# One-core decoder step: the last four projection columns in halves, two attention units begun amid them

## The chip, the cores and the metric

The kernel runs on one core of one Trainium2 chip. The time is that of the device for one execution, in microseconds (us). Names of engines: PE is the matrix unit (TensorE), PEld its weight loads, DVE VectorE, ACT ScalarE, POOL GpSimd, SP SyncE, which here issues DMA transfers. PSUM is the memory that PE writes to, eight banks of 128 x 512 floats; SBUF is the memory of the tiles.

## The reference

One step of a hybrid decoder layer, for a prompt of 1024 tokens and eight sample tokens that decode one position each, all in float32. One projection feeds three groups of heads (attention with three branches, an RWKV-7 recurrence, attention into 256 memory rows); each group is gated, and one more projection and the residual close the layer:

```python
q_raw, kv_raw, g_raw, z_nsa, u_rw, z_rw, q_mem, z_mem = split_in(rms_norm(hp, ln_g[l]) @ w_in[l])
q, rows4, rows_w = nsa_project(q_raw, kv_raw, pos_p, nsa_q_norm[l], nsa_k_norm[l])
gates = jax.nn.sigmoid(g_raw).reshape(bp, tp, NSA_HEADS, 3)
o_nsa = lax.map(lambda a: nsa_prompt_seq(*a, *cmp_params), (q, rows4, rows_w, gates))
o_rw, sh_p, st_p = rwkv7_mix(u_rw, ...)
mkv_p = mem_kv(mem_prompt, mem_norm_g[l], w_mem_kv[l], mem_k_norm[l])
o_mem = mem_attend(q_mem, mkv_p, mem_q_norm[l])
hp = hp + mixer_out(o_nsa, z_nsa, o_rw, z_rw, o_mem, z_mem, w_out[l])
```

The attention group is, for a block of 128 queries, `gate_mix(g, o_c, o_s, o_w)`: a softmax over compressed keys (`o_c`), one over selected blocks of keys (`o_s`), one over a window of 512 (`o_w`). `mem_kv` is `rms_norm(mem, g) @ w_kv`, with one more norm per head on its keys. `mixer_out` multiplies each group by `silu` of its `z` columns. The sample tokens go through the same with a cache.

## The kernel before

Products that need float32 are made from split operands: a weight block is loaded as `wraw`, ACT rounds it to `whi` and DVE subtracts to `wlo` (`w_split`, L283 and L284); three matmuls (`h`, low part of `h`, `wlo`) make one product. `wraw` and the split pair have two buffers each (pools `wr`, `wp`).

**Phase 1** multiplies the 1024 tokens with `w_in`, 128 columns at a time (`columns`, then `project`, L307). A column has two halves of tokens: H=0 with tokens 0 to 511 and the eight sample tokens (24 matmuls of 256 and 24 of 264 columns), H=1 with 512 to 1023 (24 of 512). Both use the same split block. Results land in the PSUM pool `ppr` (3 banks). The last four columns are `z` columns: `do_z` makes `zt` on ACT (L318) and DVE (L319) and writes it to `z_d` in DRAM by SP (L320). While these four run, a generator `bg`, made by `ahead`, is stepped: BG = 6 steps of it for each 8 steps of a column. `ahead` makes the compressed keys (`prompt_cmp`), the memory's keys and values (`mem_kv`: `p_mT` L1090, four raw blocks of `w_mem_kv` with their split L1099 to L1103, products `p_mo` L1110 in the PSUM pool `pw`, then a norm and transfers, L1116 to L1119), the attention keys `kh` and `kl`, and the queries `qs` of tile 7.

**Phase 2** goes over units (tile i of 128 queries, group g, head pair hp), tile 7 first, 32 units. `attn_scores` makes the scores `p_s` of two heads and two branches on PE, in the PSUM pool `pS` (2 buffers of 2 banks). `weigh` subtracts the maximum on DVE (L1356, which leaves `p` and `nm`) and takes the exponential on ACT (L1357); POOL multiplies by gate over sum (L1382). `attn_turn` transposes `p` on PE to `p_pT` (3 banks `pT`), copied to `pt` by ACT (L1327) or DVE (L1329) in turn; `attn_out` multiplies with the values. Scores run two units ahead, so the phase begins with those of units 0 and 1, `start`. Beside the units run other generators, among them `query_tasks`: for tile 7 the compressed branch `attn_cmp` (scores `p_sc`, weights `pcq` on DVE L1292 to L1304, their transpose), for each further tile the queries: `q` loaded by SP (L1254), split on ACT and POOL (`qhl`, L1259 and L1260), transposed on PE (`p_q`), copied to `qs`. `sample_tasks` makes the sample tokens' work (`s_in`, `s_x`, `p_sn`).

**Phase 3** is the output projection. The order of instructions on each engine is set by the framework's scheduler from the order of the code, with priorities (`first`, `high_priority`); on an engine they then run in that order, and each waits for what it reads and for the last use of the memory that it writes. Pools that are closed give their memory to pools opened later, so a tile can wait for the last use of another that lay there.

The two places in `phase1` and `phase2` that matter are the loop over `late` and `bg`, and `start = chain(scores(0), scores(1))`.

## Time and profile before

| | us |
|---|---|
| three runs | 965.71, 967.79, 972.04 (median 967.79) |
| the profiled execution | 966.81 |
| its span in the profile | 965.0 |
| PE busy in it | 926.7 (96 %) |
| DVE, ACT, POOL busy | 653.2, 441.6, 179.3 |
| mean granted clock of PE | 0.994 of full speed |

A row of the timeline gives start, duration, engine, line, operation, output and input with its shape; in brackets stands how long the engine had been idle before it and what ended that. The rows of PE are modelled at their ends, so those that run back to back overlap in print. L and a number is a line of the kernel.

### The profile page before, as it was taken

Reading aid. Unit: us, or ns where it says so; the run is one execution under the profiler, and the core shown is the slowest. Engines: PE = TensorE matmul, PEld = TensorE weight load, DVE = VectorE, ACT = ScalarE, POOL = GpSimd, SP = SyncE. Lnnn points to the kernel's source line nnn. Section 1 sums busy time; section 2 is a strip of 40 time slices with the busy share of each in tenths; the row PEclk is TensorE's granted clock in tenths of the full one; section 3 lists DMA queues with packets and bytes.
Section 4 is the critical chain, followed back from the end, with each engine's and each line's share of the span. In section 5 each row is a group of like instructions: output and inputs, shape, how many; then the busy total and the mean of one; then the engine's idle time right before and its main releaser. Section 6 shows DMA issues by size and latency. Waiting matters only on the chain.

```text
span 965.0 us, 24725 instructions
## 1 busy us (share of the span) xinstructions
PE 926.7 (96%) x9845; PEld 787.8 (82%) x9845; DVE 653.2 (68%) x2025; ACT 441.6 (46%) x990; POOL 179.3 (19%) x270
## 2 busy tenths in 40 slices
PE   8999999999999998999998999999999998999998
PEld 8998888868888887778886887888888877887875
DVE  6668579846593897653447765766777996457474
ACT  7564324333432332223435666567576666224321
POOL 2000000000000000000103435344355755211010
PEclk9999999999999999999999999999999999999999
DMA  8421314211331126146337425141210036976611
GB/s 273 130 66 45 90 28 128 78 48 55 88 100 36 40 77 164 46 112 153 97 99 210 144 68 180 45 140 33 61 40 14 27 110 178 326 242 211 208 71 42
DMA packets 133964, 103.82 MB, mean 108 GB/s; under 512 B 34705, under 2 KB 121240, under 8 KB 133720
## 3 DMA queue, kind: packets, MB, share of 16 engines
q1 hardware_dynamic: 128888, 90.53, 31.9%
q0 software_dynamic: 3200, 10.49, 3.0%
q8 instruction: 78, 1.28, 0.5%
q10 hardware_dynamic: 1760, 1.21, 0.4%
q14 instruction: 38, 0.31, 0.1%
HBM read 83.61 MB, written 22.78 MB: 110 GB/s over the span
## 4 chain that ended last, share of the span: by engine, by line
PE 72%; DVE 14%; ACT 5%; DMA 4%; issue 3%; SPq 1%; POOL 0%; DVEq 0%; ACTq 0%; POOLq 0%
PE p_pr L87 22%; PE p_out L87 9%; PE p_pr L307 6%; PE p_s L87 5%; PE p_pT L87 4%; PE p_o L87 4%; ACT p L1357 2%; DVE p L1356 2%; PE p_hid L87 2%; PE p_iy L87 2%; PE p_z L87 1%; PE p_it L87 1%; DVE pt L1329 1%; PE p_mo L1110 1%; PE p_tk L87 1%
## 5 line engine op out<-in xcount | busy, mean ns | idle before, releaser
L87 PE MATMUL p_pr<-h,whi 128*128 128x512 f32 (+5 forms) x1024 | 249.1, 336 | 0.0
L87 PEld LDWEIGHTS p_pr<-h,whi 128*128 128x128 f32 (+1 forms) x1024 | 162.3, 185 | 19.0 <-issue 2.8
L87 PE MATMUL p_pr<-h,wlo 128*128 128x512 f32 (+5 forms) x512 | 165.0, 325 | 0.6 <-DVE wlo L284 0.6
L1382 POOL TENSOR_SCALAR p<-p,fac,gates 128x640 f32<-128x640 f32 (+7 forms) x128 | 104.1, 825 | 107.3 <-DVE fac L1379 61.1
L1357 ACT ACTIVATE p<-p,nm 128x640 f32<-128x640 f32 (+7 forms) x128 | 93.0, 728 | 53.0 <-DVE nm L1356 46.6
L87 PEld LDWEIGHTS p_pr<-h,wlo 128*128 128x128 f32 (+1 forms) x512 | 93.9, 184 | 10.3 <-DVE wlo L284 0.8
L87 PE MATMUL p_pT<-ident,p 128*128 128x128 f32 x528 | 71.0, 279 | 4.9 <-ACT pt L1327 1.6
L1031 POOL MEMSET w2d<- 128x128 f32 x1 | 0.2, 206 | 394.2 <-PE p_yy L87 394.2
L1356 DVE CUSTOM_DVE_ANT_0 p<-p_s,bmask 128x512 f32<-128x512 f32 (+7 forms) x96 | 60.3, 661 | 18.5 <-PE p_s L87 18.0
L87 PEld LDWEIGHTS p_pT<-ident,p 128*128 128x128 f32 x528 | 57.0, 141 | 15.8 <-issue 6.4
L87 PE MATMUL p_s<-kh,qs 128*128 128x512 f32 (+3 forms) x191 | 66.8, 361 | 2.0 <-DVE nm L1356 1.9
L307 PE MATMUL p_pr<-h,whi 128*128 128x264 f32 (+2 forms) x320 | 68.6, 309 | 0.0
L87 PE MATMUL p_o<-pt,vs 128*64 128x128 f32 x1056 | 67.9, 277 | 0.4 <-DVE cat L1415 0.4
L284 DVE TENSOR_TENSOR wlo<-wraw,whi 128x1024 fp32r<-128x1024 f32 (+1 forms) x34 | 40.7, 1197 | 37.0 <-ACT whi L283 37.0
L87 PEld LDWEIGHTS p_o<-pt,vs 128*64 128x64 f32 x1056 | 57.0, 137 | 7.2 <-issue 3.8
L87 PE MATMUL p_s<-kl,qs 128*128 128x512 f32 (+3 forms) x192 | 61.3, 339 | 0.0
L283 ACT ACTIVATE whi<-wraw 128x1024 fp32r<-128x1024 f32 (+1 forms) x35 | 36.4, 1039 | 48.9 <-PE p_pr L87 36.7
L1329 DVE COPY pt<-p_pT 128x512 f32<-128x512 f32 (+1 forms) x72 | 48.3, 673 | 14.0 <-PE p_pT L87 13.3
L307 PEld LDWEIGHTS p_pr<-h,whi 128*128 128x128 f32 x320 | 51.2, 189 | 3.0 <-ACT whi L283 0.5
L87 PE MATMUL p_out<-woh,chi 128*128 128x512 f32 x128 | 51.8, 405 | 0.0
L87 PE MATMUL p_out<-woh,clo 128*128 128x512 f32 x128 | 50.2, 392 | 0.4 <-DVE clo L2267 0.4
L87 PE MATMUL p_out<-wol,chi 128*128 128x512 f32 x128 | 49.9, 390 | 0.0
(549 smaller groups left out, 1932.6 us busy)
## 6 DMA issues: line engine op xcount, KB each, us to landing
wraw<-in_w_in_dram SPq DMA_DIRECT2D x34, 512.0 KB, 3.8
pg<-in_c_pool_dram SPq DMA_DIRECT2D x32, 256.0 KB, 6.4
pg<-in_c_pool_dram SPq DMA_DIRECT2D x48, 128.0 KB, 2.2
x<-in_x_prompt_dram SPq DMA_DIRECT2D x8, 512.0 KB, 7.1
z_d<-zt SPq DMA_DIRECT2D x16, 256.0 KB, 3.0
cat<-z_d SPq DMA_DIRECT2D x8, 512.0 KB, 5.2
xres<-in_x_prompt_dram POOLq DMA_DIRECT2D x16, 256.0 KB, 3.6
out_dram<-xres POOLq DMA_DIRECT2D x16, 256.0 KB, 3.0
```

The costliest lines, as they stand in the source:

```text
L87: self.last = getattr(self.engine, op)(*a, **k)
L283: nc.scalar.activation(hi[:, :, :n], raw[:, :, :n], AF.Copy)
L284: (low or nc.vector).tensor_tensor(lo[:, :, :n], raw[:, :, :n], hi[:, :, :n].bitcast(F32), op=OP.subtract)
L307: self.last_mm = self.pe.matmul(ps[:m, :b - a], w[:, k, :m], h[k][:, a:b], start=(k == 0 and i == 0), stop=(k == 7 and i == 2))
L1031: nc.gpsimd.memset(w2d[:], 0.0)
L1110: PE.matmul(po[t][:], a, w[:, j], start=(k + j == 0 and i == 0), stop=(k + j == 7 and i == 2))
L1329: nc.vector.tensor_copy(pt[:, :n], ps[:, :n])
L1356: V.tensor_tensor_reduce(halves(x), halves(ps), m, -1.0, 3.0e38, op0=OP.add, op1=OP.min, accum_out=nm[:, h, b:b + 1])
L1357: A.activation(x, x, AF.Exp, scale=-1.0, bias=nm[:, h, b:b + 1], accum_out=sm[:, h, b:b + 1])
L1382: nc.gpsimd.tensor_scalar(x, x, f[:, h, b:b + 1], gate[:, hd + h, 1 + b:2 + b], op0=OP.mult, op1=OP.mult)
```

## The change

- `halves` replaces `columns` for the last four columns: first halves (H=0) of all four, then second halves (H=1) of all four. A column's weight block is loaded and split anew for its second half. BG becomes 9.
- The tiles of `h` for H=0 lie in a pool of their own, `hp0`. When the four first halves and `ahead` are done, that pool, `wk1` and the PSUM pool `pw` are closed. In their place are opened the PSUM pool `p7` (1 buffer of 2 banks) and `pp` (the tiles `p`), and the scores of units 0 and 1 of tile 7 are made as further steps of `bg`, amid the second halves (`scores`, UNITS = 2). `start` has nothing left of them.
- `attn_cmp` is split into `cmp_weights` (scores and weights `pcq`) and `cmp_turn` (the transpose). For tile 7 the weights are made in `ahead` (`stacked`), and so are the sample's tables. The last multiplication of `pcq` is on POOL for every tile.
- `mem_kv` ends with one copy of both halves to `mrows`, one norm over eight heads and one transfer.

PE at the end of `mem_kv`, where its products (`p_mo`) stand among those of the last column (`p_pr`). Before:

```order
L1110 MATMUL p_mo<-whi,mhi_6820 128x512
L1110 MATMUL p_mo<-wlo,mhi_6820 128x512
L1110 MATMUL p_mo<-whi,mlo_6822 128x512
L307 MATMUL p_pr<-h_0_667,whi 128x512
L307 MATMUL p_pr<-h_0_668,whi 128x512
L307 MATMUL p_pr<-h_0_667,wlo 128x512
L307 MATMUL p_pr<-h_1_670,whi 128x512
L307 MATMUL p_pr<-h_1_671,whi 128x512
L307 MATMUL p_pr<-h_1_670,wlo 128x512
L1110 MATMUL p_mo<-whi,mhi_6820 128x512 x2
```

After, with the end of the first column's second half, and the first scores behind:

```order
L308 MATMUL p_pr<-h_7_916,wlo 128x512
L1145 MATMUL p_mo<-wlo,mhi_6864 128x512
L1145 MATMUL p_mo<-whi,mlo_6866 128x512
L1145 MATMUL p_mo<-whi,mhi_6864 128x512
L1145 MATMUL p_mo<-wlo,mhi_6864 128x512
L1145 MATMUL p_mo<-whi,mlo_6866 128x512
L1145 MATMUL p_mo<-whi,mhi_6865 128x512 x2
L1145 MATMUL p_mo<-wlo,mhi_6865 128x512
L1145 MATMUL p_mo<-whi,mlo_6867 128x512
L1145 MATMUL p_mo<-wlo,mhi_6865 128x512
```

The products of the raw blocks now stand behind one another up to their end, and no `p_pr` between them.

PE where the projections end. Before, the last `p_pr` is followed by 24 matmuls of `p_s` (with `kh` and `kl` in turn) and the 17 of `p_sc`; then stands this:

```order
L87 MATMUL p_pT<-ident,p 128x128 x16
L87 MATMUL p_s<-kh_6300,qs 128x128
L87 MATMUL p_s<-kl_6301,qs 128x128
L87 MATMUL p_s<-kh_6303,qs 128x512
L87 MATMUL p_s<-kl_6304,qs 128x512
L87 MATMUL p_sn<-s_x_7272,s_in_7257 128x64
L87 MATMUL p_sn<-ident,s_in_7259 128x8 x7
L87 MATMUL p_pT<-ident,pcq 128x128 x4
```

After, from the last four matmuls of the last column on:

```order
L308 MATMUL p_pr<-h_6_913,wlo 128x512
L308 MATMUL p_pr<-h_7_916,whi 128x512
L308 MATMUL p_pr<-h_7_917,whi 128x512
L308 MATMUL p_pr<-h_7_916,wlo 128x512
L88 MATMUL p_pT<-ident,p 128x128 x8
L88 MATMUL p_q<-ident,qhl 128x128 x4
L88 MATMUL p_pT<-ident,p 128x128 x10
L88 MATMUL p_s<-kh_6303,qs 128x512
```

The scores of units 0 and 1 and `p_pT<-ident,pcq` have moved ahead of the end of the projections; `p_q` (queries of tile 6) stands eight transposes behind it.

SP at the same place: `z_d<-zt` is the write of a finished column, `q<-q_d` the load of a tile's queries. Before:

```order
L320 DMA z_d<-zt 128x512
L1129 DMA kd<-out_dram 128x4x64
L1254 DMA q<-q_d 128x768
L1129 DMA kd<-out_dram 128x4x64
L1254 DMA q<-q_d 128x768
L1118 DMA out_dram<-nr_y 128x256
L1270 DMA y_rw<-y_d 128x256
L1271 DMA cat_7205<-z_d 128x8x128
```

After:

```order
L321 DMA z_d<-zt 128x512
L1824 DMA mxv_8132<-in_cache_mem_dram 128x2x256 x2
L321 DMA z_d<-zt 128x512
L1295 DMA q<-q_d 128x768 x2
L1311 DMA y_rw<-y_d 128x256
L1312 DMA cat_7335<-z_d 128x8x128
```

Both loads of `q` stand directly behind the last `z_d`, as before one did behind `z_d` and one `kd`; what changed is the work of the other engines that surrounds it: the last `zt` and the last `z_d` come when the attention has already begun. The tile of the first `pt` behind them on ACT lies in memory that held `zt`.

The diff:

```diff
--- before.py
+++ after.py
@@ -25,10 +25,11 @@
 XT = 2
 PTB = 8
 KB = 2
+UNITS = 2
 FREE = 0
 ORDER = [4, 1, 11, 2, 3, 6, 5, 7, 13, 17, 10, 9, 15, 8, 0, 12, 14, 18, 16, 19, 20]
 EARLY = 17
-BG = 6
+BG = 9
 STEP = 0.7
 SLACK = 1.3
 AHEAD = 400
@@ -245,7 +246,7 @@
-        return [self.hp.tile([128, W], F32R, name=f"h{p}{H}_{k}") for p in range(2)]
+        return [self.hp[H].tile([128, W], F32R, name=f"h{p}{H}_{k}") for p in range(2)]
...
@@ -460,10 +461,12 @@
         with ExitStack() as ctx:
             P = lambda name, bufs, **k: ctx.enter_context(tc.tile_pool(name=name, bufs=bufs, reuse_waits="tile", **k))
             self.small = P("small", 2)
-            self.hp = P("hp", 1)
+            hp1 = P("hp1", 1)
             self.ev = P("ev", 1)
             self.wr = P("wr", 2)
             self.wp = P("wp", 2)
+            hctx = ctx.enter_context(ExitStack())
+            self.hp = hctx.enter_context(tc.tile_pool(name="hp0", bufs=1, reuse_waits="tile")), hp1
             rctx = ctx.enter_context(ExitStack())
             PR = lambda name, bufs: rctx.enter_context(tc.tile_pool(name=name, bufs=bufs, reuse_waits="tile"))
             self.tk = PR("tk", 1)
@@ -474,7 +477,8 @@
             self.rp = R("rp", 1)
             self.ppr = P("ppr", 3, space=PSUM)
             self.ptr = P("ptr", 2, space=PSUM)
-            self.pw = P("pw", 3, space=PSUM)
+            pctx = ctx.enter_context(ExitStack())
+            self.pw = pctx.enter_context(tc.tile_pool(name="pw", bufs=3, reuse_waits="tile", space=PSUM))
             self.hi, self.lo = ([], []), ([], [])
             self.pe = self.te = nc.tensor
             with ExitStack() as xctx:
@@ -553,10 +557,25 @@
             self.rwkv_close()
             rctx.close()
             self.key_pools()
-            self.wk = self.tk = P("wk1", 1)
+            wctx = ctx.enter_context(ExitStack())
+            self.wk = self.tk = wctx.enter_context(tc.tile_pool(name="wk1", bufs=1, reuse_waits="tile"))
             self.pM = Tag(self.ptr, "tr")
-            bg = self.ahead()
-            late = self.columns(cols[EARLY:])
+
+            def scores():
+                while len(self.half) < len(cols[EARLY:]):
+                    yield
+                pctx.close()
+                wctx.close()
+                hctx.close()
+                self.p7 = P("p7", 1, space=PSUM)
+                self.pp = self.kctx.enter_context(tc.tile_pool(name="pp", bufs=4, reuse_waits="tile", side="right"))
+                for n in range(UNITS):
+                    yield from self.attn_scores(7, 0, n, self.begun[n])
+                self.p7 = None
+
+            self.begun, self.half = [{} for _ in range(UNITS)], []
+            bg = chain(self.ahead(), scores())
+            late = self.halves(cols[EARLY:])
             for _ in group(late, 8):
                 for _ in islice(bg, BG):
                     pass
@@ -572,7 +591,14 @@
             yield from self.q_stack(7)
 
         self.mem_x()
-        yield from weave(chain(self.prompt_cmp(), self.mem_kv()), keys())
+        def stacked():
+            while 7 not in self.qs:
+                yield
+            self.pc7 = self.slot(3, [128, 8, 64], F32, "pcq")
+            yield from self.cmp_weights(7, self.pc7)
+            self.tables = self.sample_tables()
+
+        yield from weave(chain(self.prompt_cmp(), stacked(), self.mem_kv()), keys())
 
     def drive(self, work, fill):
 
@@ -626,6 +652,15 @@
                 yield STEP
         if rest:
             rest()
+
+    def halves(self, tiles):
+
+        for H in range(2):
+            for c0, do, j in tiles:
+                out = []
+                yield from self.project(H, *self.wblock(c0, 128), 128, out)
+                do(H, out, j)
+                self.half.append(H)
 
     def last_u(self):
         nc, O = self.nc, self.O
@@ -1109,15 +1144,21 @@
                     for i, (a, w) in enumerate(((h, wh), (h, wl), (l, wh))):
                         PE.matmul(po[t][:], a, w[:, j], start=(k + j == 0 and i == 0), stop=(k + j == 7 and i == 2))
             yield
+        m = self.slot(6, [128, 2, 512], F32, "mrows")
+        for t in range(2):
+            A.activation(m[:, t], po[t][:], AF.Copy)
+        y = m[:, :, 0:256].rearrange("p t (h d) -> p t h d", d=64)
+        sq = self.slot(7, [128, 8, 64], F32, "nr_sq")
+        A.activation(sq[:].rearrange("p (t h) d -> p t h d", t=2), y, AF.Square)
+        ss = self.small.tile([128, 8], F32, name="nr_ss", tag="nrss8")
+        V.tensor_reduce(ss[:], sq[:], axis=AX.X, op=OP.add)
+        r = self.rsqrt(self.small, ss[:], 8, 1.0 / 64, 1e-6)
+        yield
+        V.tensor_tensor(y, y, bc(r.rearrange("p (t h) -> p t h", t=2)[:, :, :, None], [128, 2, 4, 64]), op=OP.mult)
+        V.tensor_tensor(y, y, bc(self.gains[:, 5:6, None, :], [128, 2, 4, 64]), op=OP.mult)
         dst = O["mem_kv_prompt"]
-        for t in range(2):
-            d0 = bass.AP(tensor=dst.tensor, offset=dst.offset + t * 128 * 512, ap=[[512, 128], [1, 512]])
-            mv = self.slot(2 + t, [128, 256], F32, f"mv{t}")
-            A.activation(mv[:], po[t][:, 256:512], AF.Copy)
-            kn = self.norm_rope(po[t][:, 0:256].rearrange("p (t c) -> p t c", t=1), 5, 1, 4, None)
-            nc.sync.dma_start(d0[:, 0:256], kn.rearrange("p h d -> p (h d)"))
-            nc.sync.dma_start(d0[:, 256:512], mv[:])
-            yield
+        nc.sync.dma_start(bass.AP(tensor=dst.tensor, offset=dst.offset, ap=[[512, 128], [128 * 512, 2], [1, 512]]), m[:])
+        yield
 
     def mem_keys(self):
 
@@ -1272,6 +1313,18 @@
 
     def attn_cmp(self, i):
 
+        pcq = self.we.tile([128, 8, 64], F32, name="pcq", tag="pcq")
+        yield from self.cmp_weights(i, pcq)
+        yield 7.0
+        yield from self.cmp_turn(i, pcq)
+
+    def cmp_turn(self, i, pcq):
+
+        self.pcT[i] = self.pt_copy(lambda j: pcq[:, 2 * j:2 * j + 2, :].rearrange("p a b -> p (a b)"), "c")
+        yield
+
+    def cmp_weights(self, i, pcq):
+
         nc = self.nc
         V, A, G, PE = nc.vector, nc.scalar, nc.gpsimd, self.te
         qs = self.qs[i]
@@ -1286,7 +1339,6 @@
                     PE.matmul(p2[:, j, g], qs[:, 4 * g + j, :], ck[:, 0, g * 64:g * 64 + 64], start=False, stop=(j == 3 and g == 1 and n == 1))
             if j == 1:
                 yield 0.1
-        pcq = self.we.tile([128, 8, 64], F32, name="pcq", tag="pcq")
         v3 = lambda x: x.rearrange("p a b c -> p (a b) c")
         st = self.small.tile([128, 8], F32, name="c_m")
         V.tensor_reduce(st[:], v3(p2[:]), axis=AX.X, op=OP.max)
@@ -1301,10 +1353,7 @@
         V.tensor_scalar(rc[:], sm[:], 1e-30, None, op0=OP.max)
         V.reciprocal(rc[:], rc[:])
         V.tensor_tensor(gh, gh, gate[:, :, 0].rearrange("p (g h) -> p g h", g=2), op=OP.mult)
-        (G if i < 7 else V).tensor_tensor(pcq[:], pcq[:], bc(rc[:, :, None], [128, 8, 64]), op=OP.mult)
-        yield 7.0 if i < 7 else 4.0
-        self.pcT[i] = self.pt_copy(lambda j: pcq[:, 2 * j:2 * j + 2, :].rearrange("p a b -> p (a b)"), "c")
-        yield
+        G.tensor_tensor(pcq[:], pcq[:], bc(rc[:, :, None], [128, 8, 64]), op=OP.mult)
 
     def attn_rwkv(self, i):
         cat = self.cat[i]
@@ -1364,7 +1413,7 @@
                 Ps[h, b] = self.pp.tile([128, 1024 if b == 0 else 640], F32, name="p", tag=f"p{b}")
             if split:
                 for h in range(2):
-                    ps = self.pS.tile([128, 1024], F32, name="p_s", tag="s")
+                    ps = (self.p7 or self.pS).tile([128, 1024], F32, name="p_s", tag="s")
                     scores(ps[:, c0:512], qs[:, hd + h, :], b, c0, 512)
                     scores(ps[:, 512:n1], qs[:, hd + h, :], b, 512, n1)
                     weigh(ps[:, c0:n1], h, b, c0)
@@ -1468,7 +1517,7 @@
 
     def query_tasks(self):
 
-        yield from self.attn_cmp(7)
+        yield from self.cmp_turn(7, self.pc7)
         self.done.add(("cmp", 7))
         for i in range(6, -1, -1):
             while i < 6 and (self.unit < 4 * (5 - i) + 2 or ("mem", i + 2) not in self.done):
@@ -1521,7 +1570,6 @@
             self.pT = P("pT", 3, space=PSUM)
             self.pO = P("pO", 1, space=PSUM)
             self.pM = Tag(self.pT, "t")
-            self.pp = P("pp", 4)
             self.load_z(7)
             self.te = nc.tensor
             self.attn_setup(P)
@@ -1532,7 +1580,7 @@
-            P = [{} for _ in units]
+            P = self.begun + [{} for _ in units[UNITS:]]
...
@@ -1582,9 +1630,9 @@
                 lag = lambda n: n + (2 if n < 15 else 3)
                 return [m for m in range(lag(n - 1) + 1, lag(n) + 1) if m < len(units)]
 
-            start = chain(scores(0), scores(1))
-            for k in range(6):
-                next(start)
+            start = chain(*(scores(n) for n in range(UNITS, 2)))
+            for k in range(2):
+                next(start, None)
                 slot()
             pts = turn(*groups[0])
             for _ in start:
@@ -1643,7 +1691,8 @@
-        return rows[:NS, 0:896].rearrange("p (k c) -> p k c", k=7)
+        self.nc.sync.dma_start(rows[:, 896:1024], self.I["c_rw"][:, 128:256])
+        return rows[:NS, 0:896].rearrange("p (k c) -> p k c", k=7), rows[:, 896:1024]
...
@@ -1659,9 +1708,7 @@
-        sums = self.slot(1, [128, 1024], F32, "s_in1")[:, 0:128]
-        nc.sync.dma_start(sums, I["c_rw"][:, 128:256])
-        rows = self.sample_tables()
+        rows, sums = self.tables
...
```

## The prediction

> **What bounds the kernel now.** I read the page first (span and busy times), then two-microsecond windows over the place where the projections end and attention begins, then the engines' timelines there.
>
> ```profile
> span 965.0 us, 24725 instructions
> PE 926.7 (96%) x9845; PEld 787.8 (82%) x9845; DVE 653.2 (68%) x2025; ACT 441.6 (46%) x990; POOL 179.3 (19%) x270
> ```
>
> TensorE (PE) works 926.7 of 965.0 us. The change leaves PE the same matmuls, so it can move only PE's idle time and the time PE runs at a lower clock. Columns of the windows: length, then busy time and count of PE, weight load, DVE, ACT, POOL, then granted clock, DMA share, GB/s.
>
> ```profile
> 508.00:510.00 2.00, 2.00 (x11) 1.59 (x9) 0.27 (x1) 0.93 (x3) 0.00 (x0) 1.00 0.31 25
> 512.00:514.00 2.00, 2.00 (x11) 1.60 (x10) 2.00 (x16) 0.77 (x4) 0.00 (x0) 1.00 0.20 67
> 516.00:518.00 2.00, 0.99 (x9) 0.86 (x7) 1.31 (x3) 0.00 (x0) 0.00 (x0) 1.00 0.36 120
> 518.00:520.00 2.00, 1.08 (x5) 0.65 (x6) 2.00 (x5) 1.24 (x2) 0.00 (x0) 1.00 1.00 270
> 520.00:522.00 2.00, 1.90 (x6) 1.08 (x7) 1.16 (x3) 1.49 (x4) 0.73 (x1) 0.59 0.95 279
> 522.00:524.00 2.00, 2.00 (x7) 1.22 (x6) 1.91 (x6) 2.00 (x7) 1.56 (x2) 0.56 1.12 339
> 524.00:526.00 2.00, 1.83 (x14) 1.43 (x13) 2.00 (x4) 1.07 (x4) 1.52 (x2) 1.00 1.03 255
> 526.00:528.00 2.00, 2.00 (x18) 1.58 (x17) 1.89 (x7) 2.00 (x4) 1.14 (x2) 1.00 0.99 260
> 528.00:530.00 2.00, 0.29 (x5) 0.19 (x4) 2.00 (x6) 1.61 (x5) 1.81 (x3) 1.00 1.05 346
> 530.00:532.00 2.00, 1.33 (x7) 1.36 (x8) 1.93 (x6) 0.21 (x1) 1.59 (x1) 0.65 0.93 292
> 532.00:534.00 2.00, 2.00 (x9) 1.70 (x9) 1.60 (x6) 0.46 (x2) 0.00 (x0) 0.50 0.80 248
> ```
>
> The last projection matmul ends near 513.2 us. From 516 to 534 PE is busy 0.99+1.08+1.90+2.00+1.83+2.00+0.29+1.33+2.00 = 13.42 of 18 us: 4.6 us idle. In 520 to 524 it runs at 0.59 and 0.56 of its clock, in 530 to 534 at 0.65 and 0.50: lost are 1.90 x 0.41 + 2.00 x 0.44 = 1.66 and 1.33 x 0.35 + 2.00 x 0.50 = 1.47, together 3.1 us. **This seam loses 7.7 us in all**, and that is all the change can win. PE's timeline names the waits:
>
> ```profile
> 512.80 0.39 PE L307 MATMUL p_pr<-h,wlo 128*128 128x512 f32 x1
> ...
> 518.73 0.33 PE L87 MATMUL p_s<-kh,qs 128*128 128x128 f32 x1 [1.74 <-DVE nm L1356]
> ...
> 524.88 1.89 PE L87 MATMUL p_pT<-ident,p 128*128 128x128 f32 x15 [0.17 <-POOL p L1382]
> ...
> 530.67 1.09 PE L87 MATMUL p_pT<-ident,pcq 128*128 128x128 f32 x4 [2.38 <-DVE pcq L1304]
> ...
> 532.83 1.05 PE L87 MATMUL p_q<-ident,qhl 128*128 128x128 f32 x4
> ```
>
> 1.74 us goes to the scores' buffer, which the softmax weighing on DVE (`nm`) frees late; 2.38 us to `pcq`, the compressed branch's weights, made in DVE's queue amid that weighing. DVE is busy 2.00 of 2.00 us in 518 to 520 and 524 to 526: too much of its work begins at once. Before the seam it is nearly free (0.27 of 2.00 in 508 to 510), and PE full. So the change moves work from a place where DVE is the bound to a place where PE is.
>
> **The change part by part.** Durations come from these rows.
>
> ```profile
> L87 PE MATMUL p_pr<-h,wlo 128*128 128x512 f32 (+5 forms) x512 | 165.0, 325 | 0.6 <-DVE wlo L284 0.6
> L284 DVE TENSOR_TENSOR wlo<-wraw,whi 128x1024 fp32r<-128x1024 f32 (+1 forms) x34 | 40.7, 1197 | 37.0 <-ACT whi L283 37.0
> L283 ACT ACTIVATE whi<-wraw 128x1024 fp32r<-128x1024 f32 (+1 forms) x35 | 36.4, 1039 | 48.9 <-PE p_pr L87 36.7
> ...
> wraw<-in_w_in_dram SPq DMA_DIRECT2D x34, 512.0 KB, 3.8
> z_d<-zt SPq DMA_DIRECT2D x16, 256.0 KB, 3.0
> cat<-z_d SPq DMA_DIRECT2D x8, 512.0 KB, 5.2
> ...
> 481.94 0.33 PE L1147 MATMUL p_k<-ident,kd 128*128 128x128 f32 x1 [0.57 <-POOL kd L1140]
> ...
> 513.23 0.60 ACT L318 ACTIVATE zt<-p_pr 128x512 f32<-128x512 f32 x1 [1.64 <-PE p_pr L307]
> 513.72 0.22 ACT L1669 ACTIVATE s_x<-t_s 128x32 f32<-128x32 f32 x1
> 514.18 0.26 ACT L1672 ACTIVATE s_x<-s_x 128x64 f32<-128x64 f32 x1
> 520.51 0.42 ACT L1259 ACTIVATE qhl<-q 128x256 fp32r<-128x256 f32 x1 [0.56 <-DMA q<-q_d]
> 525.46 0.60 ACT L1327 ACTIVATE pt<-p_pT 128x512 f32<-128x512 f32 x1 [0.93 <-PE p_pT L87]
> ...
> 514.11 0.67 DVE L319 SCALAR_TENSOR_TENSOR zt<-zt,p_pr 128x512 f32<-128x512 f32 x1
> 517.45 1.22 DVE L1356 CUSTOM_DVE_ANT_0 p<-p_s,bmask 128x1024 f32<-128x1024 f32 x1
> 518.59 0.08 DVE L1356 DVE_READ_ACCUMULATOR2_ANT nm<- 128x1 f32 x1
> 520.34 0.81 DVE L1356 CUSTOM_DVE_ANT_1 p<-p_s,bmask 128x640 f32<-128x640 f32 x1
> ...
> 521.01 0.73 POOL L1260 TENSOR_TENSOR qhl<-q,qhl 128x256 fp32r<-128x256 f32 x1 [18.62 <-ACT qhl L1259]
> ...
> 514.14 0.35 SPq L1118 DMA_DIRECT2D out_dram<-nr_y  x1
> 514.81 0.33 SPq L320 DMA_DIRECT2D z_d<-zt  x1
> 516.58 0.39 SPq L1129 DMA_DIRECT2D kd<-out_dram  x1
> 517.02 0.50 SPq L1254 DMA_DIRECT2D q<-q_d  x1
> ```
>
> *Removed.* Both waits above go: units 0 and 1 and `pcq` are made before the projections end. With them go 4.6 us of idle and 3.1 us of slow clock: -7.7.
>
> *Four columns in halves.* Each weight block is loaded and split twice: 4 more transfers of 512 KB, 4 x 1.04 us on ACT, 4 x 1.20 us on DVE. A first half has 24 matmuls of 256 and 24 of 264 columns, a second 24 of 512 (the timeline's steps are 0.23 us), so PE's sum is unchanged and a half lasts about 5.6 us, against 1.04 + 1.20 to split. That cover holds over both passes but where other work on PE displaces it: `mem_kv`'s raw blocks 2, 3 and 4 now stand with no projection between them. A block's 12 matmuls last 2.8 us, its transfer and split 3.8 + 1.04 + 1.20 = 6.0 us with two buffers, so two blocks in 5.6 us are just short: 0.4 us here, 0.3 us more where the low half of the weights comes last, and 0.4 us for the column behind them, whose block shares the rings. Below nothing it cannot be, as PE has to have these matmuls in any order; the nearest row for the low end is 0.6 us that `wlo` cost PE over 512 matmuls, the high end a whole transfer with its split, 3.8 + 2.2 - 2.8 = 3.2 us. I take 1.1.
>
> *Scores of two units amid the second halves.* Eight score tiles pass through one buffer of PSUM. Tile n+1 waits for the weighing of n: 1.22 + 0.08 us for 1024 columns, 0.81 + 0.08 for 640, about 0.2 us more for the hand-over (518.67 to 518.73, and as much before). Between the tiles stand 8, 14, 5, 7, 7, 7 and 5 projection matmuls of 0.23 us: 1.9, 3.3, 1.2, 1.6, 1.6, 1.6, 1.2 us. Against 1.5 and 1.1 that covers each by itself, but DVE has a `wlo` of 1.20 or a norm of `mem_kv` in front of two of the weighings: 0.6 and 0.2 us. The first tile also waits for two copies of `p_mo` on ACT (2 x 0.60 us, two matmuls in between): 0.6 us. The chain before `mem_kv` (`p_sc`, small transposes) adds 0.3. Sum 1.7; the ends are 0 and eight times 0.6, as much as the 0.57 us the trace has for a like hand-over (`p_k`), 4.6.
>
> *`mem_kv`'s tail.* One norm of eight heads and one transfer instead of two and four: fewer small operations on DVE, three transfers less. PE's projections are what ends last there: nothing, and if DVE were late there, as the score sum assumes, it would give back at most the 1.22 us of one weighing. `pcq`'s last multiplication goes to POOL, which has nothing else then; it is needed ten microseconds later. `sample_tables` runs earlier on DVE and ACT and finds the free time before 510. The sample's pieces move tens of microseconds back in the attention phase, where others stand in for them: nothing.
>
> *The new seam.* Behind the last projection matmul PE has only work that waits. The transpose `p_pT` there needs a PSUM buffer freed by ACT's `pt` copy; that `pt` lies where `zt` of the last two columns lay, so it waits until both `z_d` transfers have landed. The way from PE's last matmul: ACT `zt` 0.6 us, DVE `zt` 0.67, issue on SP at about +1.4; landing 3.0 later, +4.4; `pt` 0.60, +5.1 (with hand-over). So **PE idles 5.1 us**, then does 8 transposes, 0.9 us at full clock (16 take 1.89 to 2). The next, `p_q`, needs POOL's `qhl`. SP issues `q` right behind the last `z_d`, queued behind its wait for DVE: +1.75, and 520.51 - 517.02 = 3.5 us later ACT could use it, +5.3. But ACT's queue has `pt`, `pt`, four `s_x` (0.7 us together, 513.72 to 514.44) and a third `pt` first: `qhl` starts at about +7.0, ends +7.4, POOL's 0.73 follows, `p_q` at +8.2: another 8.2 - 6.0 = 2.2 us. Idle 7.3 us together. The landing may be as short as 2.4 us (the write of `nr_y`, issued at 514.14, let `kd` go at 516.58) or as long as `cat`'s 5.2: 6.7 to 9.5 us. What else is queued behind the two `z_d` on SP, `y_rw` and `cat`, is wanted only once a unit's outputs are gated, later than `p_q`.
>
> *The clock.* After the gaps of 1.74 and 2.38 us the clock was low for some 3.5 us, beginning two to three microseconds behind the start of each gap (516.99 and 528.29), and cost 1.5 to 1.7. A gap of 7.3 us broken by 0.9 takes up part of such stretches itself; what is left is 1.4 (the transposes and the first two microseconds behind `p_q`) to 3.1 (another whole stretch). I take 2.0. The Trainium skill, "TensorE: Matmul & The Clock Gate", "HAM oscillation", has it that gaps up to about 3.4 us keep the clock. The rows above go against it, at 1.74 and 2.38 us; by the page the second gap would cost nothing and the sum be 0.6 us lower, as the first alone exceeds its bound.
>
> *Sum:* -7.7 + 1.1 + 1.7 + 7.3 + 2.0 = **+4.4 us**. The profiled execution took 966.81 us (span 965.0 and 1.8 around it), so 971.2; it lies 1.0 below the median of three, 967.79, whose runs reach from 965.71 to 972.04.
>
> **The rivals.**
> - *The new seam is shorter and nothing stalls amid the columns* (not slower): the transfers land in 2.4 us since the queues are empty there, as in 512 to 514 with a DMA share of 0.20. Then idle is 6.7 us, the clock 1.4, the rest 0.6: 8.7 - 7.7 = +1.0; if `qhl` also gets past the two copies and `s_x` (1.9 us), -0.9, and if moreover no stretch is slow, -2.3: 964.5 to 967.8. It decides at a landing of `z_d` under some 2.5 us and a `p_q` within 6 us of the last projection. For it: the empty queues. Against: `p_q` hangs on a fixed order on ACT whatever lands.
> - *Waits only change places*, the change does not do what it says: idle and slow clock add up to 7 to 9 us again, 966 to 968. For it: the old two waits and the new two are alike in number.
> - *Worse than that:* landings under load (share 0.9 to 1.1 in 518 to 530, `cat` 5.2 us), idle 9.5, clock 3.1, the raw blocks 3.2 and the scores 3.0: 18.8 - 7.7 = +11.1, 977.9. It decides when `z_d` needs over 5 us or when DVE's queue holds up more than four of the score tiles.
>
> **How the numbers follow.** Forecast (+1.5 to +8): 0.55. Shorter seam (-3 to +1): 0.20. Same loss elsewhere: 0.12. Worse (above +8): 0.13. One per cent, 9.7 us, is about what a measurement can tell here. Faster by that is more than the seam holds: 0.02. Slower by it needs most of the worst case: 0.10. The range leaves out the top of the last case and what lies below the second: 963 to 977.5.
>
> **What would show it.** `p_s<-kh` tiles among `p_pr` with waits under 1 us each; `p_pT` behind the last `p_pr` with an idle time of about 5 us put down to ACT `pt` or a DMA of `z_d`; `p_q` with about 2 us put down to POOL `qhl`; a granted clock near 0.5 just after; no wait for `pcq`. DVE should be busy over 1.2 of 2 us all through the second halves. I am wrong if `p_pT` does not wait there, if raw blocks wait more than 2 us, or if the time falls below 964.

## The result

| | median us | runs | range |
|---|---|---|---|
| before, beside these runs | 967.79 | 5 | 965.09 to 972.04 |
| after | 975.0 | 5 | 970.79 to 976.87 |

The ratio is 1.0063, 95% interval 1.0037 to 1.0089: slower, by 3.6 to 8.6 us. The profiled execution of after took 976.87 us, the slowest of its five, so its trace shows more loss (10.1 us of span) than the ratio does (6.1 us). One slow execution of all (1263.66 us at a granted clock of 0.653, whole columns with the edits on `zt` and `q`) is left out of every median and ratio below. Of the page of after, the span and the busy times:

```profile
span 975.1 us, 24716 instructions
PE 932.3 (96%) x9845; PEld 791.5 (81%) x9845; DVE 658.6 (68%) x2013; ACT 445.7 (46%) x993; POOL 181.1 (19%) x271
```

PE has the same 9845 matmuls. The waits for the scores' buffer at the seam (1.74 us) and for `pcq` (2.38 us) are gone. PE's timeline from 470 to 550 us, the rows with a wait over 0.2 us:

```profile
475.83 0.33 PE L1188 MATMUL p_k<-ident,kd 128*128 128x128 f32 x1 [0.62 <-POOL kd L1181]
480.14 0.80 PE L1145 MATMUL p_mo<-whi,mhi 128*128 128x512 f32 x1 [0.56 <-ACT mhi L1128]
496.86 0.50 PE L1145 MATMUL p_mo<-wlo,mhi 128*128 128x512 f32 x1 [0.52 <-DVE wlo L1138]
503.63 0.74 PE L308 MATMUL p_pr<-h,whi 128*128 128x512 f32 x2 [1.36 <-ACT whi L284]
504.60 0.51 PE L1395 MATMUL p_s<-kh,qs 128*128 128x512 f32 x1 [0.24 <-ACT mrows L1149]
516.33 0.33 PE L1395 MATMUL p_s<-kh,qs 128*128 128x128 f32 x1 [1.08 <-DVE nm L1405]
536.54 1.97 PE L88 MATMUL p_pT<-ident,p 128*128 128x128 f32 x8 [4.42 <-ACT pt L1376]
540.31 1.12 PE L88 MATMUL p_q<-ident,qhl 128*128 128x128 f32 x4 [1.80 <-POOL qhl L1301]
```

The last two are the new seam; the projections end at 532.1. What PE waits for there is told by the rows of ACT's timeline,

```profile
532.16 0.60 ACT L319 ACTIVATE zt<-p_pr 128x512 f32<-128x512 f32 x1 [3.48 <-PE p_pr L308]
535.89 1.08 ACT L1376 ACTIVATE pt<-p_pT 128x512 f32<-128x512 f32 x2 [3.13 <-DMA z_d<-zt]
539.04 0.71 ACT L1300 ACTIVATE qhl<-q 128x256 fp32r<-128x256 f32 x2
```

and, in the timeline of SP's queue:

```profile
533.51 0.33 SPq L321 DMA_DIRECT2D z_d<-zt  x1
533.89 0.93 SPq L1295 DMA_DIRECT2D q<-q_d  x2
```

ACT is idle for 3.13 us, until `z_d` has landed, 2.4 us behind its issue at 533.51, and `pt` can start. Behind `pt`, and behind the `s_x` and a third `pt` that stand between, comes `qhl`; and `q` was issued only behind the last `z_d`. The windows of after where PE idles or its clock falls (columns as in the prediction's windows):

```profile
478.00:480.00 2.00, 1.58 (x9) 1.17 (x8) 1.75 (x3) 0.39 (x1) 0.00 (x0) 0.55 0.01 5
480.00:482.00 2.00, 1.86 (x4) 1.39 (x5) 1.21 (x4) 0.09 (x1) 0.00 (x0) 0.50 0.89 254
482.00:484.00 2.00, 2.00 (x8) 1.68 (x7) 0.78 (x2) 1.03 (x3) 0.00 (x0) 0.50 0.43 144
484.00:486.00 2.00, 2.00 (x9) 1.48 (x9) 1.23 (x4) 0.91 (x2) 0.00 (x0) 0.75 0.00 0
...
504.00:506.00 2.00, 1.76 (x7) 1.16 (x6) 1.53 (x3) 1.97 (x4) 0.00 (x0) 0.87 0.82 254
506.00:508.00 2.00, 2.00 (x6) 1.54 (x6) 2.00 (x4) 0.90 (x2) 0.00 (x0) 0.50 0.96 259
508.00:510.00 2.00, 2.00 (x9) 1.59 (x8) 0.52 (x2) 0.50 (x2) 0.00 (x0) 0.77 0.01 3
...
532.00:534.00 2.00, 0.13 (x1) 0.00 (x0) 1.21 (x2) 0.60 (x1) 0.00 (x0) 1.00 0.01 3
534.00:536.00 2.00, 0.00 (x0) 0.00 (x0) 0.08 (x1) 0.11 (x1) 0.00 (x0) 1.00 0.80 225
536.00:538.00 2.00, 1.46 (x7) 1.46 (x8) 0.31 (x1) 1.56 (x6) 0.00 (x0) 0.55 1.00 351
538.00:540.00 2.00, 0.51 (x3) 0.11 (x1) 0.39 (x1) 1.21 (x3) 0.47 (x1) 0.50 1.09 309
540.00:542.00 2.00, 1.69 (x8) 1.69 (x9) 0.00 (x0) 0.54 (x2) 0.94 (x2) 0.50 1.10 282
542.00:544.00 2.00, 2.00 (x12) 1.87 (x11) 1.12 (x2) 0.97 (x3) 0.73 (x1) 0.74 0.07 17
```

By such windows, idle time is length less PE's busy time, clock loss is busy time times (1 - granted clock). Before, the seam lost 7.7 us. After, 532 to 544 lose 6.2 idle and 2.3 of clock, 8.5; 476 to 532 lose 3.8 idle (0.6 of it the `p_k` that before has too) and **4.8 of clock, in two slow stretches amid the columns** (3.1 and 1.7). 8.5 + 3.2 + 4.8 - 7.7 = 8.8 of the 10.1 us between the two spans. Slow stretches elsewhere come and go from run to run in every kernel here (before has one of 1.7 us at 384 to 388, after one of 1.7 at 922 to 926).

The first of the two stretches begins within the compressed scores. They start at 476.5, 0.7 us behind the wait of 0.62 us, and their steps go from 0.11 to 0.21 us at 478.2, some 1.4 us before the wait of 0.56 us begins:

```profile
477.99 0.28 PE L1339 MATMUL p_sc<-ckl,qs 128*128 128x64 f32 x1
478.10 0.33 PE L1339 MATMUL p_sc<-ckh,qs 128*128 128x64 f32 x1
478.25 0.40 PE L1339 MATMUL p_sc<-ckl,qs 128*128 128x64 f32 x1
478.46 0.40 PE L1339 MATMUL p_sc<-ckh,qs 128*128 128x64 f32 x1
```

One more number is of use below: a run's time times its mean granted clock, an estimate of its time at full clock. Its mean over the runs is 962.1 for before (25 runs beside the first experiments, mean 968.9) and 965.3 for after (5 runs, mean 974.7). So by this estimate some 3.2 us of the loss are waits, and some 2.6 clock. (For the kernel before it moved between 960.9 and 962.1 from one group of runs to the next, so a difference of about 1 us says nothing.)

### The profile page after: what moved, and what is told of

The parts are those of the page before. It is cut to its first block, busy times and chain, and to the rows that moved or that the text cites. A ratio compares the mean times of both kernels' runs of the same rounds, so it can differ in the third digit from the quotient of the medians.

```text
span 975.1 us, 24716 instructions
## 1 busy us (share of the span) xinstructions
PE 932.3 (96%) x9845; PEld 791.5 (81%) x9845; DVE 658.6 (68%) x2013; ACT 445.7 (46%) x993; POOL 181.1 (19%) x271
## 4 chain that ended last, share of the span: by engine, by line
PE 68%; DVE 16%; ACT 6%; DMA 5%; issue 3%; SPq 1%; POOL 0%; DVEq 0%; ACTq 0%; POOLq 0%
PE p_pr L88 19%; PE p_out L88 7%; PE p_pr L308 7%; PE p_s L88 4%; PE p_pT L88 4%; PE p_o L88 4%; ACT p L1406 2%; PE p_hid L88 2%; DVE p L1405 2%; PE p_iy L88 2%; DMA pg<-in_c_pool_dram 1%; PE p_z L88 1%; PE p_it L88 1%; DVE pt L1378 1%; DVE wlo L285 1%
## 5 line engine op out<-in xcount | busy, mean ns | idle before, releaser
L285 DVE TENSOR_TENSOR wlo<-wraw,whi 128x1024 fp32r<-128x1024 f32 (+1 forms) x38 | 45.9, 1207 | 42.7 <-ACT whi L284 42.7
L284 ACT ACTIVATE whi<-wraw 128x1024 fp32r<-128x1024 f32 (+1 forms) x39 | 40.6, 1041 | 54.0 <-PE p_pr L88 36.7
L88 PE MATMUL p_s<-kh,qs 128*128 128x512 f32 (+3 forms) x176 | 59.5, 350 | 0.0
L88 PE MATMUL p_s<-kl,qs 128*128 128x512 f32 (+3 forms) x176 | 54.5, 331 | 0.0
L1376 ACT ACTIVATE pt<-p_pT 128x512 f32<-128x512 f32 (+1 forms) x72 | 41.6, 582 | 21.0 <-PE p_pT L88 16.8
```

The costliest lines, as they stand in the source:

```text
L88: self.last = getattr(self.engine, op)(*a, **k)
L284: nc.scalar.activation(hi[:, :, :n], raw[:, :, :n], AF.Copy)
L285: (low or nc.vector).tensor_tensor(lo[:, :, :n], raw[:, :, :n], hi[:, :, :n].bitcast(F32), op=OP.subtract)
L1376: nc.scalar.activation(pt[:, :n], ps[:, :n], AF.Copy)
```

## The experiments

The edits are shortened; `...` and the comments stand for what is left out. Three theories at the start. A: the new seam is a chain (`z_d` lands, `pt`, `p_pT`), and beside it another (`q` is issued late, `qhl`, `p_q`). B: the time is lost amid the columns, by the single PSUM buffer and the double loading. C: only the landing of `z_d` costs. D (the clock falls behind the run of 64-column matmuls) and E (DVE's small work at the old seam) came later. Ratios are to the kernel before on the same chip.

**The compressed branch's `pt` of tile 7 in memory of its own.**

```diff
+        own = self.slot(5, [128, 4, 128], F32, "pt7") if i == 7 else None
...
+        if pt is None:                                    # pt=own for tile 7's pcq
             pt = self.wk.tile([128, 4, 128], F32, name="pt", ...)
```

> The changed kernel with one tile moved: the transposed compressed weights of tile 7 (pt) lie in memory of their own, not where zt lay. Theory A (the end of the projections is a chain z_d, pt, p_pT, and beside it a chain q, qhl, p_q): the wait of 4.42 us for ACT pt goes, but the load of q still stands behind the last z_d on SP, so p_q waits until about 6.5 us behind the last projection; idle there falls only from 6.2 to about 5.5 us and the slow stretch behind it stays: 0 to 2 us faster than the changed kernel. Theory B (what is lost is lost amid the columns, by single buffering and double loading): no difference at all, and p_q not waited for longer than before. Theory C (the landing of z_d alone is what costs): 5 to 7 us faster.

Measured: 973.72 us, ratio 1.0038 (1.0015 to 1.0062). Its PE waits from 470 to 550 us:

```profile
PE p_q L88 <- POOL qhl L1301: 4.6, 1, 4.6
PE p_pr L308 <- ACT whi L284: 1.4, 1, 1.4
PE p_pT L88 <- ACT pt L1378: 1.3, 1, 1.3
```

4.42 for `pt` became 1.3, and 1.8 for `qhl` became 4.6: 5.9 of 6.2 us are still there, and the time is 1.3 us lower by the medians, within the 0 to 2 expected. That is A; C falls, since with the landing of `z_d` out of `pt`'s way nearly all stays.

**The same, with the load of tile 6's queries amid the second halves.**

```diff
+                self.q6 = self.slot(4, [128, 12, 64], F32, "q6")
+                nc.sync.dma_start(self.q6[:]..., self.q_d[6 * 128:7 * 128, :])
                 pctx.close()
```

> The same, and the load of tile 6's queries is issued amid the second halves, ahead of the last z_d. Theory A: p_q about 2 us behind the last projection, idle there about 1.5 us instead of 6.2, no slow clock there (2.3 us): 6 to 7 us faster than the changed kernel, about as fast as the kernel before, up to 2 us slower. Theory B: at most 2 us faster than the changed kernel.

Measured: 970.42 us, ratio 1.0021 (0.9996 to 1.0046): 3 to 5 us better, not 6 to 7. The wait for `p_q` is gone, and another has come; its row in PE's waits, and below it the row of DVE's timeline:

```profile
PE p_pT L88 <- DVE pt L1385: 4.5, 1, 4.5
```

```profile
531.99 1.29 DVE L1385 COPY pt<-p_pT 128x512 f32<-128x512 f32 x2 [2.39 <-DMA z_d<-zt]
```

With one `pt` moved away, the pool put the next one, DVE's, where `zt` had lain. At full clock the time is 964.5 us, against 965.3: by that estimate the waits are as long as in the changed kernel, and what was won is clock (1.4 us lost between 440 and 560 us in this profile, 7.1 there). Here, moving the tile that waits only passed the wait on; the next experiment moves the one that is waited for.

**The last column's `zt` in memory of its own, and the early load.**

```diff
-        t = self.ev.tile([128, 520], F32, name="zt", tag="ev", bufs=2)
+        t = self.slot(5, [128, 520], F32, "zt7") if H and row == ... else self.ev.tile(...)    # the last column's row
```

> The changed kernel with the last column's zt in memory of its own (so no tile of the attention waits for the landing of z_d) and the load of tile 6's queries ahead of the last z_d. Theory A: behind the last projection PE idles under 1.5 us instead of 6.2 and no slow clock follows from it; the waits amid the columns (3.8 us) stay. At full clock 5 us less than the changed kernel, with the slow stretch of 2.3 us up to 7 less: 967 to 970 beside 974 to 975. Theory B (a wait of the same length appears at the next step, as in the two kernels before, because DVE or ACT is late): idle there stays above 4 us, 971 or more.

Measured: 964.57 us, ratio 0.9966 (0.9946 to 0.9986): faster than the kernel before, and some 10 us faster than the changed one; both theories had it at 967 or more. From 520 to 548 PE is idle 0.08 us by the windows; its timeline where the projections end has no wait at all:

```profile
530.03 0.39 PE L308 MATMUL p_pr<-h,wlo 128*128 128x512 f32 x1
530.26 1.04 PE L88 MATMUL p_pT<-ident,p 128*128 128x128 f32 x8
531.13 0.60 PE L88 MATMUL p_q<-ident,qhl 128*128 128x128 f32 x4
```

At full clock (time times granted clock, mean of 12 runs) it takes 959.6 us against 965.3, 5.7 less: the 6.2 us of idle time. A is confirmed at its full price for the waits, and B falls as their main cause: the waits amid the columns (0.56, 0.54, 0.80, 0.52 and 1.07 us in its trace) are still there. The rest of the 10 us is clock: the slow stretches at the seam and at 504 to 510 us are not in this profile, the one at 478 to 485 is (3.1 us). No run has `zt` moved without the early load, so the two edits' shares are not told apart.

**No unit early, halves kept.**

```diff
-UNITS = 2
+UNITS = 0          # and six steps of start, as before
```

> The changed kernel with no unit begun early: halves, early compressed weights and the rest stay, the scores of units 0 and 1 follow the projections as in the kernel before. Theory A: the scores cover z_d and q, the wait for pcq stays away, that for the scores' buffer (1.7 us) returns; amid the columns the waits of p_mo and whi (2.4 us) and their slow clock (about 4.8 us) stay: 3 to 5 us faster than the changed kernel. Theory B (early units are what stalls the columns): slow clock amid the columns goes as well, 7 to 9 us faster than the changed kernel.

Measured: 972.05 us, ratio 1.0035 (1.0013 to 1.0056): about 3 us better than the changed kernel, the low end of A, and not clear of noise (the intervals overlap, and at full clock it takes 965.2 us, against 965.3). The 7 to 9 us of B did not come. The wait for `p_q` is 4.2 us there, the scores do not cover it, since the scheduler now has `p_q` stand ahead of the second unit's scores. The column's `whi` is waited for as long (1.6 us), and the clock falls behind it as before.

**Whole columns, no unit early; early weights, tables and single norm stay.**

```diff
-UNITS = 2
+UNITS = 0          # and BG = 6, pools and start as before
...
-            late = self.halves(cols[EARLY:])
+            late = self.columns(cols[EARLY:])
```

> Whole columns again, as in the kernel before, with no unit begun early; what stays of the change are the compressed weights of tile 7 and the sample's tables ahead of the memory's products, and the single norm. Theory A: the wait for pcq (2.38 us) and its slow clock (1.5 us) go, the raw blocks of the memory stand among projections again: 2 to 4 us faster than the kernel before. Rival: the small products of the compressed scores, now ahead of a chain of transposes, slow the clock there as in the changed kernel (3.1 us): no faster than the kernel before.

Measured: 974.43 us, ratio 1.0056 (1.0037 to 1.0075). That was expected faster than before, and is as slow as the changed kernel with no half and no early unit in it. The slow stretch that the rival named is there (486 to 490 us, 1.7 us), and PE has two long waits at the seam:

```profile
PE p_q L88 <- POOL qhl L1302: 3.2, 1, 3.2
PE p_s L88 <- DVE nm L1406: 2.6, 1, 2.6
```

ACT's and DVE's timelines tell what stood ahead of them:

```profile
518.05 0.60 ACT L319 ACTIVATE zt<-p_pr 128x512 f32<-128x512 f32 x1
521.84 0.60 ACT L1377 ACTIVATE pt<-p_pT 128x512 f32<-128x512 f32 x1 [3.19 <-DMA z_d<-zt]
...
523.30 1.15 ACT L1407 ACTIVATE p<-p,nm 128x1024 f32<-128x1024 f32 x1 [0.25 <-DVE nm L1406]
...
526.83 0.42 ACT L1301 ACTIVATE qhl<-q 128x256 fp32r<-128x256 f32 x1 [1.14 <-DMA q<-q_d]
```

```profile
521.43 0.69 DVE L1158 TENSOR_TENSOR mrows<-mrows,rq_r 128x512 f32<-128x512 f32 x1
522.04 1.22 DVE L1406 CUSTOM_DVE_ANT_0 p<-p_s,bmask 128x1024 f32<-128x1024 f32 x1
```

`pt` of the early weights stands right behind the last `zt` and waits 3.19 us for its `z_d`, as A has it. But the exponential behind it started only 1.5 us later, when DVE had the maximum (`nm`): the weighing stood behind the memory's single norm on DVE until 522.04, and that is the 2.6 us. The 3.2 us are `q`, issued behind that `z_d` and two other loads at 521.17, for which `qhl` waited. So of A's two links the late `q` costs PE time here; that the wait of `pt` does is not shown.

In the kernel before, `pt` of `pcq` stood where `z_d` had long landed, because `pcq` came late.

**The same, with the two edits on `zt` and `q`.** (The edit on `zt` as above; the load of `q` at the end of `mem_kv`.)

> Whole columns, no early units, early compressed weights (974.4 us without the next two edits), now with the last zt in memory of its own and tile 6's queries loaded ahead of the last z_d. Theory A: what early weights cost there was their pt copy on ACT, which waited 3.2 us for the landing of z_d with the exponentials queued behind it, and q; both go: 9 to 12 us faster than with them, 962 to 965, with the slow stretch behind the run of compressed scores still there (1.7 us). Theory D alone (the slow clock of that run is what costs): at most 3 us faster, 971 or more.

Measured: 963.82 us, ratio 0.9961 (0.9936 to 0.9986), some 10 us faster than without. The time lies in A's range, but the profile does not show A as the reason for most of it. The wait for `q` is gone, that for a score buffer has grown to 3.7 us (the norm still stands in front of the weighing on DVE), and the 40 us behind the last projection lose 6.3 us idle and 1.6 of clock, without the edits 7.8 and 3.4: 3.3 of the 12.3 us between the two spans. The last projection itself ends 3.7 us earlier (513.95, without the edits 517.61), the slow stretch of 1.7 us behind the compressed scores, which was expected to stay, is gone, and a wait of 2.1 us for a transfer of the sample's work at 594 us as well. What cost the kernel with early weights the rest stays open.

**Early units and halves, weights late again.**

```diff
-            yield from self.cmp_weights(7, self.pc7)          # in ahead
-        yield from self.cmp_turn(7, self.pc7)                 # in query_tasks
+        yield from self.attn_cmp(7)
```

> The changed kernel with the compressed scores and weights of tile 7 back at the start of the attention; halves and early units stay. Theory D (a run of matmuls with only 64 columns counts as idle for the clock: 16 of them, 1.9 us, and waits of 0.6 us on both sides are what slowed the clock at 478 to 485): no slow stretch between 476 and 490. Rival (the waits of 0.6 us alone do it): the stretch stays. At the end of the projections pcq is waited for again: idle there 5 to 8 us. Time as the changed kernel within 3 us either way.

Measured: 980.31 us, ratio 1.013 (1.0096 to 1.0164), 5 us slower than the changed kernel, beyond the 3 expected. At the seam `p_pT` waits for `pt` as in the changed kernel, and then for `pcq`:

```profile
PE p_pT L88 <- POOL pcq L1354: 4.9, 1, 4.9
PE p_pT L88 <- ACT pt L1374: 4.4, 1, 4.4
```

So with the units early, the early weights win 5 us or a little more. No stretch is slow between 476 and 490 us here, as D had it; but the wait of 0.56 us behind the compressed scores is gone with them, so the rival is not ruled out by this:

```profile
478.00:480.00 2.00, 2.00 (x12) 1.60 (x10) 1.54 (x3) 1.46 (x4) 0.00 (x0) 1.00 0.00 0
480.00:482.00 2.00, 2.00 (x13) 1.41 (x11) 1.68 (x5) 1.36 (x3) 0.00 (x0) 1.00 0.57 131
```

**Whole columns, no early units, weights late: the tables, the single norm, and POOL's product stay.** (The edits for whole columns and for late weights together.)

> Whole columns, no early units, compressed weights at the start of the attention: of the change there stay the sample's tables ahead of the memory's products, the single norm with its one transfer, and the product of pcq on POOL. Theory: as the kernel before within 1.5 us, as none of this lies on the path. Rival: the kernel with whole columns and early weights was slow because of the single norm (its keys are loaded later, and what is queued on SP behind that, z_d and q): 3 to 6 us slower than before here too, with q waited for at the seam.

Measured: 962.79 us, ratio 0.9947 (0.9926 to 0.9967). Both expectations miss: what was priced at nothing wins 5 us. Its two parts apart, on the kernel before:

```diff
+            self.tables = self.sample_tables()       # in ahead, instead of in sample_setup
```

> The kernel before with one part of the change alone: the sample's tables are made ahead of the memory's products, so DVE's ten or so operations on s_in leave 512 to 515.4. Theory E (what stood in DVE's way at the seam was the memory's norms and the tables, 509.7 to 517.4, and that is what whole columns with late weights won 5 us by): half or more of the 1.74 us wait for the scores' buffer goes, with or without its slow stretch: 1 to 4 us faster than before. Rival (only both together, or only the norm, matter): within 1 us of before.

```diff
-        for t in range(2):                            # two norms of four heads, four transfers
+        m = self.slot(6, [128, 2, 512], F32, "mrows") # one of eight, one transfer
```

> The kernel before with another part alone: one norm over eight heads and one transfer at the end of the memory's keys. Theory E: the second half of that norm ran on DVE at 516.65, behind a wait of 1.05 us for a transfer to let its memory go, and the scores' weighing stood behind it; with the single norm that wait goes and the weighing begins about a microsecond earlier: 1 to 5 us faster than before. Rival: within 1 us of before, as the tables fill that time.

Measured: the early tables alone 961.51 us, ratio 0.9944 (0.9923 to 0.9965); the single norm alone 965.40, ratio 0.9979 (0.9957 to 1.0001), which can't be told from no gain. The tables alone win as much as both together, and more than the 1 to 4 us expected. (For the tables the edit also gives the memory's values `mv` another place and loads one small tile, `c_rw`, earlier.) At full clock it is 958.9 us, against 960.9 for the kernel before beside it: some 2 us of the gain are waits, the rest clock. DVE's timeline at the seam in the kernel before has nine operations on `s_in` from 512.02 to 515.6, of 0.24 us each, in between those of the norm and in front of the weighing at 517.45; the first, the last, and the norm's end:

```profile
512.02 0.24 DVE L1642 TENSOR_TENSOR s_in<-gains,rope 8x96 f32<-8x96 f32 x1
...
515.36 0.24 DVE L1645 TENSOR_SCALAR s_in<-s_in 8x192 f32<-8x192 f32 x1
516.65 0.42 DVE L383 TENSOR_TENSOR nr_y<-p_mo,rq_r 128x256 f32<-128x256 f32 x1 [1.05 <-DMA out_dram<-nr_y]
517.11 0.42 DVE L384 TENSOR_TENSOR nr_y<-nr_y,gains 128x256 f32<-128x256 f32 x1
```

With the tables early none of them stands there:

```profile
515.15 0.42 DVE L383 TENSOR_TENSOR nr_y<-p_mo,rq_r 128x256 f32<-128x256 f32 x1 [1.13 <-DMA out_dram<-nr_y]
515.61 0.43 DVE L384 TENSOR_TENSOR nr_y<-nr_y,gains 128x256 f32<-128x256 f32 x1
515.96 1.22 DVE L1361 CUSTOM_DVE_ANT_0 p<-p_s,bmask 128x1024 f32<-128x1024 f32 x1
```

The projections end 0.5 us earlier there (last product at 512.27, before at 512.80), the weighing begins 1.5 us earlier, and the transpose of `pcq` 3.1 us (527.58, before 530.67), without a wait of its own. The wait for the scores' buffer falls from 1.74 to 0.77 us, and 510 to 538 lose 2.6 us idle and 1.5 of clock, 4.1 instead of 7.7. The norm's wait for its transfer is as long as before (1.13 us, 1.05), only earlier. The single norm alone does not get there: its first weighing stands at 518.18, held 0.97 us by a DMA, again `z_d<-zt`, since the first `p` tile lies there too.

**The compressed scores split in three runs**, on the kernel with `zt` in its own memory.

```diff
+                if i == 7:
+                    for _ in range(3):
+                        yield            # after each pair of p_sc; BG = 12
```

> The kernel with zt in memory of its own and q early, and the 16 compressed scores of 64 columns no longer in one run: 9 of them, 13 projection matmuls, 6 of them, 24 projection matmuls (one stands ahead). Theory D (a run of such matmuls slows the clock whether or not PE is shown busy): no slow stretch at 478 to 485, which cost 3.2 us there: 961 to 963, against 964.6. Rival (the stretch comes from where the waits fall in the clock's windows): it stays in the profile or appears elsewhere amid the columns, 964 to 966.

Measured: 963.88 us, ratio 0.9963 (0.9943 to 0.9983), against 964.57: no gain that can be told. The profiled run has a granted clock of 1.00 throughout and no slow stretch, though PE waits there for 0.68 and 0.89 us (475 and 487 us); other runs of it have 0.994. At full clock it takes 961.4 us, against 959.6: what the clock gave, longer waits took (7.9 us idle between 440 and 560 us in the profiles, against 5.6).

**One more run of 16 products of 64 columns**, on the kernel with early tables. These products are the compressed scores over again, and nothing reads them.

```diff
+            p2 = self.pM.tile([128, 4, 2, 64], F32, name="p_sx", tag="m")
+            for j in range(4):
+                for g in range(2):
+                    for n, ck in enumerate((self.ckh, self.ckl)):
+                        self.te.matmul(p2[:, j, g], self.qs[7][:, 4 * g + j, :], ck[:, 0, g * 64:g * 64 + 64], ...)
```

> The kernel before with early tables (961.5 us), and added to it 16 more products of 64 columns amid the projections, where PE is full: the compressed scores once more into memory that nothing reads. Theory D: they take 1.8 us themselves, and the clock falls behind them, for 1.5 to 3.2 us more: 964 to 966.5, a slow stretch right behind them in the profile in most runs, mean clock lower by 0.002 to 0.003. Rival (only waits slow the clock): 1.8 us and no more, 963.3, no slow stretch there.

Measured: 964.74 us, ratio 0.997 (0.995 to 0.999); by the medians 3.2 us more than without, by the ratios 2.5, with intervals that overlap, so an excess over the 1.8 us of the run itself is not clear of noise. No stretch is slow behind the run in the profile (1.00 in every window from 476 to 492), and the mean granted clock over the runs is the same, 0.997 in both. Of the 6.1 us between the two profiled spans (966.0 and 959.9), 1.0 is idle time at the seam (512 to 540: 3.6 us, without the run 2.6), 1.8 the run, and some 3.4 more slow clock far from it, at 690 and 814 us. D is not shown: a run of small matmuls beside a wait of 0.6 us is not enough.

## Why the prediction was right, and where it was off

The time lies in the range, and the sign and the likeliest case (+1.5 to +8) held by the runs: +6 to +7 us, +4.4 forecast. The profiled pair, +10.1, lies where the prediction put its worst case, though neither of that case's conditions held (`z_d` landed in 2.4 us, and DVE held up one score tile, by 1.08 us). That the sum came within 2 or 3 us of the runs is in part luck: the largest loss that the profile shows beside the new seam, slow clock amid the columns, had no term. Term by term, against the profiled execution:

| term | forecast | measured |
|---|---|---|
| the old seam's loss goes | -7.7 | -7.7 |
| halves, raw blocks | 1.1 | 0.52 + 1.36 = 1.9 |
| scores amid the columns, chain before | 1.7 | 0.56 + 0.24 + 1.08 = 1.9 |
| idle at the new seam | 7.3 | 4.42 + 1.80 = 6.2 |
| clock there | 2.0 | 2.3 |
| clock amid the columns | not in the sum | 4.8 |
| sum | +4.4 | +9.4 of the 10.1 (8.8 by the windows) |

- *Removed waits*: right, both are gone. But they did not need the units moved, and the prediction did not ask whether they did. They were long because DVE had the tables and norms in front of the weighing, and moving the tables alone won 5 to 6 us.
- *Four columns in halves* and *scores of two units*: the places were right (a raw block's low half, the column behind it, one score tile), the sizes within a microsecond. That score tile waited behind a norm of `mem_kv` on DVE (`mrows`, 1.58 us from 513.95), one of the two rows that the prediction named for it. The windows, without the 0.6 us of `p_k`, give 3.2 us idle for both terms, against 2.8 forecast. One sign that was announced did not come: DVE is not busy over 1.2 of 2 us all through the second halves (0.52 at 508 to 510 us, 0.92 at 518 to 520, next to nothing from 528 on).
- *`mem_kv`'s tail and the tables* is where the reading failed: "finds the free time before 510" is so, but the step did not ask what the tables had held up in the place that they leave. It took the norm for nothing because PE's projections end last there, with at most 1.22 us if DVE were late, and gave the tables no price; its own window 512 to 514 has DVE busy 2.00 of 2.00 us with 16 operations, and these stood in front of the weighing, on which PE waits next. In the changed kernel this gain is part of the -7.7 and does not count twice.
- *The new seam*: right in both links and in order. The landing was the short one, 2.4 us, as the rival had it (the DMA share is 0.01 when `z_d` is issued); that is 0.7 of the 1.1 us less. The rival's other condition, `p_q` within 6 us, did not hold: it came at +8.2 as forecast (532.1 to 540.31), and waited 0.4 us less only because the eight transposes ahead of it took 1.97 us at slow clock, not 0.9.
- *The clock* is the term that was mis-sized. A sum that gave a price to slow clock at the seam gave none to the waits amid the columns, though the prediction's own rows had gaps of 1.74 us costing 1.66. The 1.36 us behind the raw blocks, with 0.24 next to it, cost 1.7. The two experiments in which that wait is about as long (1.4 and 1.6 us: own `pt`, no early units) have the stretch too, the two in which it is 0.7 and 0.8 (`q` early, `zt` own) do not. The other stretch, 478 to 485, cost 3.1. It begins within the compressed scores and before the wait of 0.56 us, so that wait did not start it. The Trainium skill, "TensorE: Matmul & The Clock Gate", "HAM oscillation", would have gaps up to about 3.4 us keep the clock; the traces here do not agree, at 1.36 us.
- *The range*: it is wide, 963 to 977.5, and held because it made room for the worst case; the slowest run of the five, 976.87, lies near its end, and the likeliest case's own sum was 2 to 3 us low of the runs.

What stays open is when a stretch becomes slow. The one at 478 to 485 is in the profiles of the changed kernel and of four experiments with early, unbroken compressed scores (`pt` own, no early units, whole columns with early weights, `zt` own), and in none of those with late or split ones; but two with early, unbroken ones do not have it either, and the run that was added on another kernel did not make one. Waits that add up do not settle it either: with early tables, waits of 0.77, 0.19 and 0.40 us (517 to 520) stand ahead of a slow stretch of 1.5 us, and in the kernel with the added run 0.63, 0.19 and 0.38 us at the same place do not.
